# A hybrid encoder step on one core: the first norm moved onto the token-major rows, and the residual turned beside the first gate

## Chip, core and metric

The kernel runs on one NeuronCore of a Trainium2 chip. TensorE (PE) multiplies matrices and transposes, VectorE (DVE), ScalarE (ACT) and GpSimd (POOL) work elementwise, and SyncE (SP) issues nearly all DMAs. The metric is the device time of one execution in microseconds (us). All data are float32; products are made from operands split into a high and a low float32r part.

## What is computed

One step of one layer over 336 tokens (16 meta tokens, 256 of a prompt, 64 of a sample), each a row of 2048 numbers:

```python
u = _rmsnorm(x, norm_mix_w)
z_a, xbc_a, dt_a, qkv_b, z_b, beta_b, a_b, gate_a, gate_b = jnp.split(u @ w_in, SPLIT_IDX, axis=-1)
# ya: SSD mixer with causal conv; ob: gated DeltaNet with causal conv; both chunked scans
mix = (jax.nn.sigmoid(gate_a) * (ya.astype(xd) @ w_out[:SSD_D_INNER])
       + jax.nn.sigmoid(gate_b) * (ob.astype(xd) @ w_out[SSD_D_INNER:]))
h = x + mix
hid = jnp.square(jax.nn.relu(_rmsnorm(h, norm_mlp_w) @ w_up))
h = h + hid @ w_down
```

where `_rmsnorm` divides each token's row by its root mean square and multiplies by a weight per channel. Conv and scan states come out too, and the rows of `h` after a last norm.

## The kernel before

**Layout.** `u` is kept channel-major: 16 tiles `k` of 128 channels (partitions) by 336 tokens, as a high part `uh` and a low part `ul`. The weights stream past it: `w_in`, then `w_out`, `w_up`, `w_down`, in chunks `n` of 512 rows by 256 columns (`raw`, 512 KB each, three buffers). `wload(n)` issues the DMA of a chunk three chunks ahead, `wsplit(n)` makes `hi` on ACT and `lo = raw - hi` on DVE (for chunk 3 on POOL). The buffer of chunk n+3 is free when `lo` of chunk n is done. `block` multiplies two column tiles of 128 by `u`: four chunks, in each 4 `k` by 2 columns by 3 products (hi·uh, lo·uh, hi·ul), into two PSUM tiles `pbig`. So one block over `u` is 96 products of 336 columns.

**Order.** PE runs its instructions in the order in which the code issues them. From `manual` to `manual.close()` all engines do. Elsewhere a scheduler orders the other engines and the DMA queue of SP ahead of time; each engine then runs its fixed list, and SP stands still at a DMA whose condition isn't met, with all later DMAs behind it. The DMAs share eight completion counters in turn, so a DMA also waits until the eighth before it has landed.

**Start.** The token rows come as three tiles `x0` to `x2` of 112 rows by 2048. For each, a sum of squares (`sumsq`) and a root (`root`, its power on POOL) give one factor per token; PE transposes the raw `x` (`flip`, 48 transposes of 112 columns) into `xT`. The factors are spread over all partitions by three small products (`prx`, `rbx`), each `k` is scaled from `xT` into `ut` (`u_scale`, DVE and POOL by turns) and split with the norm weight (`u_split`: `uh` on ACT, `ul` on DVE). The first block runs beside this, two generator steps for each `k`.

**Behind the first block** come, in PE's order, six transposes `pcol` of conv weights and states (`cra`, `crb`, `sra`, `srb`) and 32 products `ptok` with the 64 columns for time step, beta and decay (`wt`, loaded by two DMAs of 128-byte runs, split into `wtr` by ACT and DVE). The loads `cra` to `wt` go into the pool `sp`, which is opened when `xp`, the pool of `x0` to `x2`, is closed, in the same space. So they wait for the last reader of `x`. `dvec` (two DMAs of 4-byte elements, 64 by 16) has its own space. `scratch` writes the channel-major residual from `xT` to DRAM (`xTd`, 16 DMAs of 160 KB) and zeroes four DRAM scratch tensors (`aD`, `uD`, 12 DMAs of 258 KB) that the second mixer's scans use, from about 580 us on.

**First gate.** Beside the first scan of the second mixer (`scan_gdn(0)`), `gate_a` runs 8 blocks. For each of 16 tiles it reads `xTd` back (`xr`), takes the sigmoid on ACT, multiplies by `acc` on DVE, adds `xr` on POOL, and stores to `hAd`, where `gate_b` takes it later.

Of the kernel before, what the change touches and what calls it, by code (L numbers as in the profile page):

```python
# [42 lines left out]
def tile_hybrid_step(ctx: ExitStack, tc: tile.TileContext, i: dict, o: dict):  # L43
    nc = tc.nc
# [9 lines left out]
    def scr(name):  # L54
        return pss.tile([P, 512], F32, tag="sc", name=name)

    def mm(out, lhsT, rhs, start=True, stop=True, **kw):
        nc.tensor.matmul(out, lhsT=lhsT, rhs=rhs, start=start, stop=stop, **kw)  # L58

    def act(out, in_, func=AF.Copy, **kw):  # L60
        nc.scalar.activation(out=out, in_=in_, func=func, **kw)  # L61

    def tt(eng, out, a, b, op):
        eng.tensor_tensor(out=out, in0=a, in1=b, op=op)  # L64

    def stt(out, a, s, b, op0, op1):
        nc.vector.scalar_tensor_tensor(out=out, in0=a, scalar=s, in1=b, op0=op0, op1=op1)  # L67

    V, G = nc.vector, nc.gpsimd
# [15 lines left out]
    def transp(out, in_):  # L85
        n = in_.shape[0]
        nc.tensor.transpose(out, in_, ident[:n, :n])
# [32 lines left out]
    NM, SN, NP_, CB_, GN = 0, 16, 32, 48, 72  # L120

    rowd = dpool.tile([2, 48, NT], F32, name="rowd")
    xTd = dpool.tile([KD, P, NO], F32, name="xTd")
    hAd = dpool.tile([KD, P, NO], F32, name="hAd")

    DG = P * P + P
# [66 lines left out]
    def wload(n):  # L193
        if n >= len(stream) or n in raws:
            return
        raw = wpool.tile([P, 4, 256], F32, tag="raw", name="raw", bufs=3)
        for c0, src in stream[n]:
            nc.sync.dma_start(raw[:, :, c0:c0 + src.shape[1]], src.rearrange("(k p) c -> p k c", p=P))
        raws[n] = raw

    def wsplit(n):
        if n >= len(stream) or n in split:
            return
        wload(n)
        hi = wpool.tile([P, 4, 256], F32R, tag="hi", name="hi", bufs=3)
        act(hi, raws[n])
        lo = wpool.tile([P, 4, 256], F32R, tag="lo", name="lo", bufs=3)
        tt(G if n == 3 else V, lo, raws[n], hi.bitcast(F32), SUB)
        split[n] = hi, lo

    used, hold = [0], [len(stream)]
# [46 lines left out]
    def proj(n0=0, n1=None):  # L258
        return (yield from block(KD, umov, (n0, n0 if n1 is None else n1), NT))
# [25 lines left out]
        G.memset(t, 0.0)  # L285
    xctx = ExitStack()
    xp = xctx.enter_context(tc.tile_pool(name="xp", bufs=1))
    xs = []
    segs = [[(0, "meta", 0, 16), (16, "pr", 0, 96)], [(0, "pr", 96, 112)], [(0, "pr", 208, 48), (48, "sa", 0, 64)]]
    src = {"meta": i["meta_tokens"], "pr": i["x_prompt"][0], "sa": i["x_sample"][0]}  # L290
    def load_x(n):
        for p0, s, r0, nr in segs[n]:
            nc.sync.dma_start(xs[n][p0:p0 + nr, :], src[s][r0:r0 + nr, :])

    for n in range(3):
        xs.append(xp.tile([112, D], F32, name=f"x{n}"))
    load_x(0)
    load_x(1)
    prow = sp0.tile([73, P], F32, name="prow")
    for r0, name, nr in ((NM, "norm_mix_w", 16), (SN, "ssd_norm_w", 16), (NP_, "norm_mlp_w", 16), (CB_, "ssd_conv_b", 24), (GN, "gdn_norm_w", 1)):  # L300
        nc.sync.dma_start(prow[r0:r0 + nr, :], i[name][0].rearrange("(t c) -> t c", c=P))
    load_x(2)
    warm = sp0.tile([P, 1], F32, name="warm")
    act(warm, ones[:, 0:1], AF.Square)

    def load_cols(dst, row, n):
        ps = scr("pcol")
        transp(ps[:, :n], row[:n, :])
        V.tensor_copy(dst, ps[:, :n])


    xT = [cpool.tile([P, 4, NT], F32, tag=t, name="xT", bufs=b) for t, b in (("q", 2), ("k", 2), ("v", 1))]
    xT.append(sp0.tile([P, 4, NT], F32, name="xT3"))
    junk = acc.rearrange("p k n -> p (k n)")[:112, :]
    ssx = sp0.tile([112, 4], F32, name="ssx")
    rsx = sp0.tile([112, 3], F32, name="rsx")
    dgx = sp0.tile([112, 3, 112], F32, name="dgx")
    rbx = sp0.tile([P, NT], F32, name="rbx")
    HD = D // 2

    def sumsq(f, x, d0, n):
        d = junk[:, d0:d0 + x.shape[1]]
        if f is act:
            act(d, x, AF.Square, accum_out=ssx[:, n:n + 1])
        else:
            V.scalar_tensor_tensor(out=d, in0=x, scalar=1.0, in1=x, op0=MUL, op1=MUL, accum_out=ssx[:, n:n + 1])

    def flip(n, k):
        ps = scr("pu").rearrange("p (k t) -> p k t", k=4)[:, :, :112]
        for m in range(4):  # L330
            transp(ps[:, m, :], xs[n][:, (k + m) * P:(k + m + 1) * P])
        return xT[k // 4][:, :, n * 112:(n + 1) * 112], ps

    def root(n):
        r = rsx[:, n:n + 1]
        V.tensor_scalar(out=r, in0=ssx[:, n:n + 1], scalar1=1.0 / D, scalar2=EPS, op0=MUL, op1=ADD)
        tt(G, r, r, nhalf_pow[:112, 0:1], ALU.pow)

    def spread_d(n):
        V.tensor_scalar(out=dgx[:, n, :], in0=ident[:112, :112], scalar1=rsx[:, n:n + 1], scalar2=None, op0=MUL)  # L340

    manual = ExitStack()
    manual.enter_context(tc.manual_schedule())

    pw_ = scr("pwarm")
    for n in range(8):
        mm(pw_[:, :P], ident, ident)
    prx = psb.tile([P, 512], F32, tag="big", name="prx")
    sumsq(act, xs[0], 0, 0)
    for k in range(0, KD, 4):  # L350
        (V.tensor_copy if k < 8 else act)(*flip(0, k))
    root(0)
    sumsq(V, xs[1], D, 1)
    for k in range(0, KD, 4):
        act(*flip(1, k))
    root(1)
    load_cols(par, prow, 73)
    for n in range(3):
        wload(n)
    sumsq(act, xs[2][:, :HD], 0, 2)  # L360
    sumsq(V, xs[2][:, HD:], D, 3)
    tt(V, ssx[:, 2:3], ssx[:, 2:3], ssx[:, 3:4], ADD)
    root(2)
    spread_d(0)
    spread_d(1)
    act(*flip(2, 0))
    late = [flip(2, k) for k in (4, 8, 12)]
    spread_d(2)
    wsplit(0)
    for n in range(3):  # L370
        mm(prx[:, n * 112:(n + 1) * 112], ones[:112, :], dgx[:, n, :])
    act(rbx, prx[:, :NT])
    for a in late:
        act(*a)
    xctx.close()
    sp = start.enter_context(tc.tile_pool(name="sp", bufs=1))

    ut = {}

    def u_scale(k):  # L380
        ut[k] = sp0.tile([P, NT], F32, tag="ut", name="ut", bufs=6)
        tt(G if k % 2 else V, ut[k], xT[k // 4][:, k % 4, :], rbx, MUL)

    def u_split(k):
        t, w = ut.pop(k), par[:, NM + k:NM + k + 1]
        act(uh[:, k, :], t, AF.Copy, scale=w)
        stt(ul[:, k, :], t, w, uh[:, k, :].bitcast(F32), MUL, SUB)

    def ctile(tag, name, bufs):
        return cpool.tile([P, 4, NT], F32, tag=tag, name=name, bufs=bufs)

    def ftile(name):
        return fpool.tile([P, 340], F32, tag="c", name=name, bufs=NC_)[:, :NO]
# [63 lines left out]

    main0 = kept(proj_ssd(0), tiles0)  # L460
    hold[0] = 0
    for k in range(4):
        u_scale(k)
    for k in range(KD):
        u_split(k)
        if k + 4 < KD:
            u_scale(k + 4)
        if k % 4 == 1 and k < KD - 4:
            wsplit(k // 4 + 1)
        for _ in range(2 if k < KD - 1 else 1):  # L470
            next(main0)
    manual.close()
# [522 lines left out]

    def scratch():

        for k in range(KD):
            nc.sync.dma_start(xTd[k], xT[k // 4][:, k % 4, NMETA:])
            yield 1.0  # L1000
        for n in range(2):
            for t in (aD, uD):
                for c in range(3):
                    nc.sync.dma_start(t[n][c].rearrange("h (p r) -> (h p) r", r=4 * DG // P), zero)

    def chain(*gens):
        for g in gens:
# [2 lines left out]
    def gate_a():  # L1010
        done = []

        def store():
            nc.sync.dma_start(hAd[done[0][0]], done.pop(0)[1])

        for b in range(8):
            pt = yield from proj(NMETA)
            for j in range(2):
                k = b * 2 + j
                xr = ftile("xr")  # L1020
                nc.sync.dma_start(xr, xTd[k])
                sgt = ftile("sgt")
                act(sgt, pt[j][:, :NO], AF.Sigmoid)
                tt(V, sgt, sgt, acc[:, k, :], MUL)
                tt(G, sgt, sgt, xr, ADD)
                done.append((k, sgt))
                if len(done) > 1:
                    store()
        store()
# [221 lines left out]
```

## Time and profile before

| | us |
|---|---|
| three runs | 2331.46, 2333.14, 2334.69 |
| median | 2333.14 |
| the profiled execution: its own time | 2331.78 |
| span, from the first to the last instruction | 2330.1 |
| TensorE's mean granted clock | 0.994 of full speed |

The profile is of one execution, and its times count from the start of the span. The page gives busy times and the groups of instructions. The chain that ended last is followed back from the last instruction, and its pieces stand in order of time. The stretches give busy times and the granted clock between two times. The timelines list instructions with their start and length, and "idle before" with what ended it. A matmul's length overlaps with the next one's; what one costs is the distance of two starts. Of TensorE's clock a row shows 1.00 (2.4 GHz) or 0.50 (1.2 GHz).

### The profile page before, as it was taken

The numbers are of one execution on the slowest core, as the hardware profiler recorded it, in microseconds if no ns is written. First come the engines' busy times: TensorE is split into PE (matmuls) and PEld (weight loads), VectorE is DVE, ScalarE is ACT, GpSimd is POOL, SyncE is SP. The second block draws the span as 40 slices with busy tenths as digits, with TensorE's granted clock in tenths as the row PEclk, the third lists the DMA queues.
The fourth block names the chain that finished last, engine by engine and source line by source line (L and its number), as shares of the span: only waits on it lengthen the run. The fifth ranks groups of instructions, "written<-read, shape, count | busy, mean of one in ns | idle before, by whom it ended". The sixth has DMA issues, their size and how long they took to land.

```text
span 2330.1 us, 40632 instructions
## 1 busy us (share of the span) xinstructions
PE 2300.5 (99%) x16393; PEld 2278.1 (98%) x16393; DVE 1360.9 (58%) x2147; ACT 1064.6 (46%) x1830; POOL 333.0 (14%) x488
## 2 busy tenths in 40 slices
PE   7999999999999999999999999999999999999997
PEld 7999999999999999999999999999999999999997
DVE  6674858585865547658668467444444444444444
ACT  5655546455445545554554445433343244324433
POOL 3151505041211102212212110000000000000000
PEclk8999999999999999999999999999999999999999
DMA  7846555545575555555546644544554444445543
GB/s 194 225 121 188 143 159 150 159 135 173 156 200 170 148 164 139 154 150 144 156 148 165 170 142 145 154 149 151 148 154 149 150 148 151 154 146 153 168 141 117
DMA packets 411046, 362.87 MB, mean 156 GB/s; under 512 B 48329, under 2 KB 407834, under 8 KB 410394
## 3 DMA queue, kind: packets, MB, share of 16 engines
q1 hardware_dynamic: 410746, 360.15, 53.1%
q8 instruction: 128, 2.10, 0.4%
q14 instruction: 60, 0.49, 0.1%
q10 hardware_dynamic: 112, 0.13, 0.0%
HBM read 340.57 MB, written 19.66 MB: 155 GB/s over the span
## 4 chain that ended last, share of the span: by engine, by line
PE 91%; DVE 5%; DMA 2%; issue 1%; SPq 1%; ACT 0%; ACTq 0%; POOL 0%; DVEq 0%
PE pbig L58 84%; DVE lo L64 1%; PE po L58 1%; DMA em<-rowd 1%; DVE pr L64 1%; DVE ubt L858 1%; PE pS L58 0%; PE pw L58 0%; PE pyd L58 0%; DVE c L67 0%; PE pkk L58 0%; PE pqk L58 0%; PE ph L58 0%; DMA x<-in_x_sample_dram 0%; PE pyo L58 0%
## 5 line engine op out<-in xcount | busy, mean ns | idle before, releaser
L64 DVE TENSOR_TENSOR lo<-raw,hi 128x1024 fp32r<-128x1024 f32 x591 | 739.1, 1251 | 697.3 <-ACT hi L61 688.0
L61 ACT ACTIVATE hi<-raw 128x1024 fp32r<-128x1024 f32 x592 | 626.3, 1058 | 892.1 <-PE pbig L58 834.6
L58 PE MATMUL pbig<-uh,hi 128*128 128x320 f32 (+2 forms) x2176 | 688.9, 317 | 3.1 <-ACT uh L61 3.1
L58 PE MATMUL pbig<-ul,hi 128*128 128x320 f32 (+2 forms) x2176 | 681.9, 313 | 2.9 <-DVE ul L67 2.7
L58 PE MATMUL pbig<-uh,lo 128*128 128x320 f32 (+2 forms) x2176 | 680.8, 313 | 1.6 <-DVE lo L64 1.6
L58 PEld LDWEIGHTS pbig<-uh,hi 128*128 128x128 f32 x2176 | 410.9, 189 | 9.1 <-ACT uh L61 3.8
L58 PEld LDWEIGHTS pbig<-ul,hi 128*128 128x128 f32 x2176 | 410.8, 189 | 4.7 <-DVE ul L67 4.3
L58 PEld LDWEIGHTS pbig<-uh,lo 128*128 128x128 f32 x2176 | 411.0, 189 | 2.4 <-DVE lo L64 2.4
L58 PE MATMUL pbig<-hh,hi 128*128 128x320 f32 x1024 | 318.0, 311 | 0.0
L58 PE MATMUL pbig<-hnl,hi 128*128 128x320 f32 x1024 | 317.1, 310 | 0.0
L58 PE MATMUL pbig<-hl,hi 128*128 128x320 f32 x1024 | 316.3, 309 | 0.0
L58 PE MATMUL pbig<-hh,lo 128*128 128x320 f32 x1024 | 316.2, 309 | 0.0
L58 PE MATMUL pbig<-hnh,lo 128*128 128x320 f32 x1024 | 315.8, 308 | 0.0
L58 PE MATMUL pbig<-hnh,hi 128*128 128x320 f32 x1024 | 315.1, 308 | 0.0
L58 PEld LDWEIGHTS pbig<-hnh,lo 128*128 128x128 f32 x1024 | 192.9, 188 | 0.0
L58 PEld LDWEIGHTS pbig<-hl,hi 128*128 128x128 f32 x1024 | 192.6, 188 | 0.0
L58 PEld LDWEIGHTS pbig<-hh,hi 128*128 128x128 f32 x1024 | 192.6, 188 | 0.0
L58 PEld LDWEIGHTS pbig<-hnh,hi 128*128 128x128 f32 x1024 | 192.4, 188 | 0.2
L58 PEld LDWEIGHTS pbig<-hh,lo 128*128 128x128 f32 x1024 | 192.5, 188 | 0.0
L58 PEld LDWEIGHTS pbig<-hnl,hi 128*128 128x128 f32 x1024 | 192.2, 188 | 0.0
L58 PE MATMUL pbig<-yh,hi 128*128 128x320 f32 x512 | 161.1, 315 | 0.0
L58 PE MATMUL pbig<-yh,lo 128*128 128x320 f32 x512 | 157.5, 308 | 0.0
(303 smaller groups left out, 2425.8 us busy)
## 6 DMA issues: line engine op xcount, KB each, us to landing
raw<-in_w_in_dram SPq DMA_DIRECT2D x256, 512.0 KB, 3.8
raw<-in_w_up_dram SPq DMA_DIRECT2D x128, 512.0 KB, 3.8
raw<-in_w_down_dram SPq DMA_DIRECT2D x128, 512.0 KB, 3.4
raw<-in_w_out_dram SPq DMA_DIRECT2D x64, 512.0 KB, 3.4
raw<-in_w_in_dram SPq DMA_DIRECT2D x32, 256.0 KB, 3.1
em<-rowd SPq DMA_DIRECT2D x8, 512.0 KB
u<-uD SPq DMA_DIRECT2D x4, 768.0 KB, 7.1
eab<-rowd SPq DMA_DIRECT2D x8, 336.0 KB, 6.9
```

The lines of the kernel that those rows point to most:

```text
L58: nc.tensor.matmul(out, lhsT=lhsT, rhs=rhs, start=start, stop=stop, **kw)
L61: nc.scalar.activation(out=out, in_=in_, func=func, **kw)
L64: eng.tensor_tensor(out=out, in0=a, in1=b, op=op)
L858: V.tensor_reduce(out=ubt[:NE, j0:, s], in_=v, axis=AX.X, op=ADD)
```

## The change

The norm is made in place on the rows of `x`, before the transposes. `scale(n, q)` multiplies a quarter (512 columns) of `x` tile `n` by the factor of each token, `x0` on ACT, `x1` and `x2` on DVE. `u_tile(k)` transposes the three scaled pieces of tile `k` into one PSUM tile and makes `uh` and `ul` from it. Three tiles are made before the first block; the others are made in it, three tiles ahead of the products. `xT`, `ut`, `rbx`, `prx` and `xTd` go. The rows of norm weights (`prow`) are loaded from ACT's queue. Ten products on the identity and four of 512 columns on raw `x` stand ahead on PE (`warmer`). `lo` of chunk 3 moves from POOL to DVE. `xp` is closed, and `sp` opened, after the 31 steps of the first block instead of before them. In `gate_a` each block loads its 256 columns of the raw rows again (three DMAs into `xr`), transposes them on PE (six transposes for each block), and DVE adds them from PSUM in place of POOL.

```diff
-        tt(G if n == 3 else V, lo, raws[n], hi.bitcast(F32), SUB)
+        tt(V, lo, raws[n], hi.bitcast(F32), SUB)
...
+        nc.scalar.dma_start(prow[r0:r0 + nr, :], i[name][0].rearrange("(t c) -> t c", c=P))
+    for n in range(3):
         for p0, s, r0, nr in segs[n]:
             nc.sync.dma_start(xs[n][p0:p0 + nr, :], src[s][r0:r0 + nr, :])
     for n in range(3):
+        wload(n)
...
+    def warmer(n, mov):
+        ps = scr("pwarm")
+        for _ in range(n):
+            mm(ps[:, :mov.shape[1]], ident[:mov.shape[0], :], mov)
...
+    def scale(n, q):
+        x, r = xs[n][:, q * QD:(q + 1) * QD], rsx[:, n:n + 1]
+        if n == 0:
+            act(x, x, AF.Copy, scale=r)
+        else:
+            V.tensor_scalar(out=x, in0=x, scalar1=r, scalar2=None, op0=MUL)
+
+    def u_tile(k):
+        ps = scr("pu")
+        for n in range(3):
+            transp(ps[:, n * XW:(n + 1) * XW], xs[n][:, k * P:(k + 1) * P])
+        w = par[:, NM + k:NM + k + 1]
+        act(uh[:, k, :], ps[:, :NT], AF.Copy, scale=w)
+        stt(ul[:, k, :], ps[:, :NT], w, uh[:, k, :].bitcast(F32), MUL, SUB)
...
-    xctx.close()
-    sp = start.enter_context(tc.tile_pool(name="sp", bufs=1))
...
+    LEAD = 3
+    warmer(10, ident)
+    for n in range(2):
+        warmer(2, xs[n][:, 3 * QD:])
+    sumsq(0)
+    root(0)
+    sumsq(1)
+    scale(0, 0)
+    root(1)
+    sumsq(2)
+    scale(1, 0)
+    root(2)
+    load_cols(par, prow, 73)
+    wsplit(0)
+    scale(2, 0)
+    for k in range(LEAD):
+        u_tile(k)
     for k in range(KD):
-        u_split(k)
-        if k + 4 < KD:
-            u_scale(k + 4)
+        if k % 4 == 0 and k < KD - 4:
+            for n in range(3):
+                scale(n, k // 4 + 1)
+        if k + LEAD < KD:
+            u_tile(k + LEAD)
+        for _ in range(2 if k < KD - 1 else 1):
+            next(main0)
         if k % 4 == 1 and k < KD - 4:
             wsplit(k // 4 + 1)
-        for _ in range(2 if k < KD - 1 else 1):
-            next(main0)
     manual.close()
+    xctx.close()
+    sp = start.enter_context(tc.tile_pool(name="sp", bufs=1))
...
-        for k in range(KD):
-            nc.sync.dma_start(xTd[k], xT[k // 4][:, k % 4, NMETA:])
-            yield 1.0
         for n in range(2):
             for t in (aD, uD):
                 for c in range(3):
                     nc.sync.dma_start(t[n][c].rearrange("h (p r) -> (h p) r", r=4 * DG // P), zero)
+                    yield 1.0
...
+            xr = ctile("qk"[b % 2], "xr", 2).rearrange("p k n -> p (k n)")
+            for m, (src_, r0, n) in enumerate(rows):
+                nc.sync.dma_start(xr[:n, m * 256:(m + 1) * 256], src_[r0:r0 + n, b * 256:(b + 1) * 256])
             pt = yield from proj(NMETA)
             for j in range(2):
                 k = b * 2 + j
-                xr = ftile("xr")
-                nc.sync.dma_start(xr, xTd[k])
+                px = scr("px")
+                for m, (_, _, n) in enumerate(rows):
+                    transp(px[:, m * P:m * P + n], xr[:n, m * 256 + j * P:m * 256 + (j + 1) * P])
                 sgt = ftile("sgt")
                 act(sgt, pt[j][:, :NO], AF.Sigmoid)
                 tt(V, sgt, sgt, acc[:, k, :], MUL)
-                tt(G, sgt, sgt, xr, ADD)
+                tt(V, sgt, sgt, px[:, :NO], ADD)
```

The scheduler also orders SP's list anew. Before, from the second `dvec` on, SP's queue in the first block reads:

```order
L488 DMA dvec<-in_ssd_d_dram 64x16x1
L490 DMA pb<-in_ssd_dt_bias_dram 128x32
L198 DMA raw<-in_w_in_dram 128x4x256
L491 DMA pb<-in_gdn_dt_bias_dram 128x16
L492 DMA pb<-in_ssd_a_log_dram 128x32
L493 DMA pb<-in_gdn_a_log_dram 128x16
L503 DMA wt<-in_w_in_dram 128x16x32
L198 DMA raw<-in_w_in_dram 128x4x256
L504 DMA wt<-in_w_in_dram 128x16x32
L198 DMA raw<-in_w_in_dram 128x4x256
```

The first `dvec`, `cra`, chunk 3 (`raw`), `crb`, `sra` and `srb` stand ahead of these rows, and the 16 `xTd` and 12 zeroing DMAs behind them. In the changed kernel the same queue reads, from behind chunks 0 to 2 on:

```order
L469 DMA dvec<-in_ssd_d_dram 64x16x1 x2
L197 DMA raw<-in_w_in_dram 128x4x256
L982 DMA aD_106<-zero 128x516 x3
L982 DMA uD_108<-zero 128x516 x3
L982 DMA aD_107<-zero 128x516
L197 DMA raw<-in_w_in_dram 128x4x256
L982 DMA aD_107<-zero 128x516 x2
L982 DMA uD_109<-zero 128x516 x2
L197 DMA raw<-in_w_in_dram 128x4x256
L982 DMA uD_109<-zero 128x516
L197 DMA raw<-in_w_in_dram 128x4x256
L457 DMA cra<-in_ssd_conv_w_dram 96x128
```

Both `dvec` now stand ahead of chunk 3 (the first `raw` here), and all 12 zeroing DMAs and chunks 4 to 6 ahead of `cra`; `crb`, `sra`, `srb`, four `pb` and both `wt` follow it, 12 DMAs in all.

On PE, the first products before and what stands ahead of them:

```order
L87 MATMUL pu<-ident,x_147 128x112 x16
L58 MATMUL prx<-dgx,ones 128x112 x3
L58 MATMUL pbig<-uh,hi 128x336
L58 MATMUL pbig<-uh,lo 128x336
L58 MATMUL pbig<-ul,hi 128x336
```

In the changed kernel 12 transposes stand ahead of the first product, and three (of `x0`, `x1`, `x2`) ahead of each later group of six, 12 times:

```order
L58 MATMUL pbig<-uh,hi 128x336
L58 MATMUL pbig<-uh,lo 128x336
L58 MATMUL pbig<-ul,hi 128x336
L87 MATMUL pu<-ident,x_144 128x112
L87 MATMUL pu<-ident,x_145 128x112
L87 MATMUL pu<-ident,x_146 128x112
L58 MATMUL pbig<-uh,hi 128x336
```

The transposes that stood in one piece ahead of the block now stand between its products. `pcol` and `ptok` follow the block in both.

## Rows read from the trace of the kernel before

**Rows 1.** The page, parts 1 and 4: busy time of engines; shares of the chain

```profile
PE 2300.5 (99%) x16393; PEld 2278.1 (98%) x16393; DVE 1360.9 (58%) x2147; ACT 1064.6 (46%) x1830; POOL 333.0 (14%) x488
...
PE 91%; DVE 5%; DMA 2%; issue 1%; SPq 1%; ACT 0%; ACTq 0%; POOL 0%; DVEq 0%
```

**Rows 2.** The chain that ended last, to 54 us: start, length, what

```profile
6.89 8.00 DMA x<-in_x_sample_dram
...
16.59 0.95 ACT hi L61
...
17.57 1.24 DVE lo L64
...
40.03 5.85 DMA wt<-in_w_in_dram
...
46.65 1.29 DVE wtr L64 x2
...
48.59 4.99 PE ptok L58 x32
```

**Rows 3.** Timeline of PE, 15 to 26 us: start, length, instruction, idle before

```profile
15.03 3.22 PE L87 MATMUL pu<-ident,x 112*128 112x112 f32 x16 [2.58 <-DMA x<-in_x_sample_dram]
...
21.84 0.65 PE L58 MATMUL pbig<-uh,hi 128*128 128x336 f32 x1 [2.30 <-ACT uh L61]
...
25.54 0.48 PE L58 MATMUL pbig<-ul,hi 128*128 128x336 f32 x1
25.82 0.48 PE L58 MATMUL pbig<-uh,hi 128*128 128x336 f32 x1
```

**Rows 4.** Stretches of the first block: length, busy us (count), PEclk, DMA, GB/s

```profile
21.84:28.20 6.36, 6.12 (x19) 5.26 (x20) 6.36 (x9) 5.19 (x9) 4.09 (x4) 0.50 0.43 117
28.20:38.50 10.30, 7.62 (x48) 7.06 (x47) 10.30 (x11) 3.04 (x5) 7.40 (x5) 1.00 0.18 43
38.50:45.20 6.70, 5.95 (x22) 5.41 (x21) 2.76 (x7) 2.11 (x5) 0.00 (x0) 0.50 1.11 189
```

**Rows 5.** Operations on DVE in the first block, and a scaling at the kernel's end

```profile
L67 DVE SCALAR_TENSOR_TENSOR ul<-ut,par,uh 128x336 fp32r<-128x336 f32 x16 | 12.3, 798 | 2.6 <-ACT uh L61 2.4
...
L1217 DVE TENSOR_SCALAR yt<-yt,frs x3: 748/752/753, 2319.2 to 2320.7; 128x1024 f32<-128x1024 f32 x2, 64x1024 f32<-64x1024 f32 x1
```

**Rows 6.** Timeline of SP's queue: start, length, DMA

```profile
11.60 0.69 SPq L488 DMA_DIRECT2D dvec<-in_ssd_d_dram  x1
...
26.45 0.61 SPq L488 DMA_DIRECT2D dvec<-in_ssd_d_dram  x1
...
28.28 0.39 SPq L198 DMA_DIRECT2D raw<-in_w_in_dram  x1
```

**Rows 7.** DMA: `dvec` to landing; packets of 28.4:36, 45.5:52 and 56:60

```profile
DMA to landing us min/median/max: 12.0/13.4/14.8
...
DMA packets 809, 0.01 MB, mean 1 GB/s; under 512 B 803, under 2 KB 809, under 8 KB 809
...
DMA packets 2229, 2.48 MB, mean 382 GB/s; under 512 B 210, under 2 KB 2229, under 8 KB 2229
...
DMA packets 1510, 1.02 MB, mean 255 GB/s; under 512 B 42, under 2 KB 1505, under 8 KB 1509
```

**Rows 8.** Timeline of PE at 684 us: four transposes between products

```profile
684.07 0.60 PE L87 MATMUL pv<-ident,v 128*80 128x128 f32 x4
684.42 0.39 PE L58 MATMUL pbig<-uh,hi 128*128 128x320 f32 x1
684.65 0.31 PE L58 MATMUL pbig<-ul,hi 128*128 128x320 f32 x1
684.80 0.31 PE L58 MATMUL pbig<-uh,lo 128*128 128x320 f32 x1
```

**Rows 9.** The first gate: a stretch (columns as in rows 4); a wait of PE

```profile
627.00:660.00 33.00, 33.00 (x228) 33.00 (x227) 30.91 (x46) 15.36 (x20) 6.64 (x5) 1.00 0.65 189
...
PE pbig L58 <- DVE lo L64: 0.2, 1, 0.2
```

More of the change, by code (lines that the diff above doesn't have):

```diff
@@ L122, in tile_hybrid_step @@
     rowd = dpool.tile([2, 48, NT], F32, name="rowd")
-    xTd = dpool.tile([KD, P, NO], F32, name="xTd")
     hAd = dpool.tile([KD, P, NO], F32, name="hAd")
@@ L287, in tile_hybrid_step @@
     xp = xctx.enter_context(tc.tile_pool(name="xp", bufs=1))
-    xs = []
+    XW = NT // 3
     segs = [[(0, "meta", 0, 16), (16, "pr", 0, 96)], [(0, "pr", 96, 112)], [(0, "pr", 208, 48), (48, "sa", 0, 64)]]
     src = {"meta": i["meta_tokens"], "pr": i["x_prompt"][0], "sa": i["x_sample"][0]}
-    def load_x(n):
+    xs = [xp.tile([XW, D], F32, name=f"x{n}") for n in range(3)]
+    HD, QD = D // 2, D // 4
+    manual = ExitStack()
+    manual.enter_context(tc.manual_schedule())
+    warm = sp0.tile([P, 1], F32, name="warm")
+    act(warm, ones[:, 0:1], AF.Square)
+    prow = sp0.tile([73, P], F32, name="prow")
+    for r0, name, nr in ((NM, "norm_mix_w", 16), (SN, "ssd_norm_w", 16), (NP_, "norm_mlp_w", 16), (CB_, "ssd_conv_b", 24), (GN, "gdn_norm_w", 1)):
+        nc.scalar.dma_start(prow[r0:r0 + nr, :], i[name][0].rearrange("(t c) -> t c", c=P))
+    for n in range(3):
         for p0, s, r0, nr in segs[n]:
@@ L295, in tile_hybrid_step @@
     for n in range(3):
[L296 to L304, printed above, removed]
+        wload(n)
     def load_cols(dst, row, n):
@@ L309, in load_cols @@
         V.tensor_copy(dst, ps[:, :n])
[L312 to L332, printed above, removed]
+    def warmer(n, mov):
+        ps = scr("pwarm")
+        for _ in range(n):
+            mm(ps[:, :mov.shape[1]], ident[:mov.shape[0], :], mov)
+    junk = acc.rearrange("p k n -> p (k n)")[:XW, :]
+    ssx = sp0.tile([XW, 6], F32, name="ssx")
@@ L334, in root, with sumsq @@
+    rsx = sp0.tile([XW, 3], F32, name="rsx")
+    def sumsq(n):
+        for m in range(2):
+            x, d, t = xs[n][:, m * HD:(m + 1) * HD], junk[:, m * HD:(m + 1) * HD], ssx[:, 2 * n + m:2 * n + m + 1]
+            if m == 0:
+                act(d, x, AF.Square, accum_out=t)
+            else:
+                V.scalar_tensor_tensor(out=d, in0=x, scalar=1.0, in1=x, op0=MUL, op1=MUL, accum_out=t)
     def root(n):
         r = rsx[:, n:n + 1]
-        V.tensor_scalar(out=r, in0=ssx[:, n:n + 1], scalar1=1.0 / D, scalar2=EPS, op0=MUL, op1=ADD)
@@ L337, in root @@
[L337 to L371, printed above, removed]
@@ L372, in tile_hybrid_step @@
-    act(rbx, prx[:, :NT])
-    for a in late:
-        act(*a)
-    xctx.close()
-    sp = start.enter_context(tc.tile_pool(name="sp", bufs=1))
[L378 to L387, printed above, removed]
+        tt(V, r, ssx[:, 2 * n:2 * n + 1], ssx[:, 2 * n + 1:2 * n + 2], ADD)
@@ new lines, in root @@
+        V.tensor_scalar(out=r, in0=r, scalar1=1.0 / D, scalar2=EPS, op0=MUL, op1=ADD)
+        tt(G, r, r, nhalf_pow[:XW, 0:1], ALU.pow)
+    def scale(n, q):
+        x, r = xs[n][:, q * QD:(q + 1) * QD], rsx[:, n:n + 1]
+        if n == 0:
+            act(x, x, AF.Copy, scale=r)
+        else:
+            V.tensor_scalar(out=x, in0=x, scalar1=r, scalar2=None, op0=MUL)
[6 more added lines that the diff above has]
+        stt(ul[:, k, :], ps[:, :NT], w, uh[:, k, :].bitcast(F32), MUL, SUB)
@@ L461, in tile_hybrid_step @@
     hold[0] = 0
-    for k in range(4):
-        u_scale(k)
-    for k in range(KD):
-        u_split(k)
-        if k + 4 < KD:
-            u_scale(k + 4)
+    LEAD = 3
[15 more added lines that the diff above has]
+        u_tile(k)
+    for k in range(KD):
+        if k % 4 == 0 and k < KD - 4:
[5 more added lines that the diff above has]
+            next(main0)
         if k % 4 == 1 and k < KD - 4:
             wsplit(k // 4 + 1)
-        for _ in range(2 if k < KD - 1 else 1):
-            next(main0)
     manual.close()
+    xctx.close()
+    sp = start.enter_context(tc.tile_pool(name="sp", bufs=1))
     hold[0] = len(stream)
@@ L1014, in store @@
             nc.sync.dma_start(hAd[done[0][0]], done.pop(0)[1])
+        rows = [(i["x_prompt"][0], 0, P), (i["x_prompt"][0], P, P), (i["x_sample"][0], 0, NSA)]
         for b in range(8):
+            xr = ctile("qk"[b % 2], "xr", 2).rearrange("p k n -> p (k n)")
+            for m, (src_, r0, n) in enumerate(rows):
+                nc.sync.dma_start(xr[:n, m * 256:(m + 1) * 256], src_[r0:r0 + n, b * 256:(b + 1) * 256])
             pt = yield from proj(NMETA)
```

## The prediction

> **What bounds the kernel now.** I read the page first. PE is busy 99% of the span and makes up 91% of the chain that ended last [rows 1], so nearly every microsecond outside PE is free, and two kinds of places count: those where PE waits, and those where PE itself gets more or less to do. The chain in order of time then shows that waits stand only at the start. Up to 14.89 us it is the loading of `x` (6.89 + 8.00), and at the end of the first block it is `wt`: issued at 40.03, landed at 45.88 (40.03 + 5.85), split by 47.94 (46.65 + 1.29); then, behind the last `pcol`, `ptok` starts at 48.59 and takes 4.99 [rows 2]. From there on the chain is PE's own work. So the first thing to ask of a change at the start is not when the first block ends but when `ptok` starts.
>
> The timeline and the stretches show the block in between. Its first product starts at 21.84, 6.95 us after `x` has landed [rows 2, 3]. The clock is at 0.50 for 6.36 us, at 1.00 for 10.30, and at 0.50 again for 6.70 [rows 4]. A product of 336 columns costs 0.28 us at half clock (25.54 to 25.82) [rows 3] and 0.156 at full clock (4.99 / 32) [rows 2].
>
> **The change, part by part.**
>
> *Until the first product.* The bytes of `x` are the same, and the last DMA of `x` had been issued 3 us before the second tile landed, so I leave its landing at 14.9. Behind it come, as before, half sums of squares, a root, and `hi` and `lo` of chunk 0, which before were done at 18.81 (17.57 + 1.24) [rows 2]; I leave that at 18.4, as DVE's sum is no longer. Behind `lo` on DVE stands the scaling of `x2`'s quarter: half of the 0.75 of 1024 columns, 0.4 [rows 5]. That is 18.8. Then the last transpose of tile 0 and nine more ahead of the first product, at 3.22 / 16 = 0.2 us each: 20.8 [rows 3]. Gain: 1 us, between 0 and 3.
>
> *The first block.* Each `k` costs six products and, for 12 of them, three transposes: 6 x 0.28 + 3 x 0.2 = 2.3 us at half clock. At full clock a transpose costs 0.11: four of them delay the second product behind them from 684.07 + 0.15 to 684.65, by 0.43 [rows 8]. So 6 x 0.156 + 3 x 0.11 = 1.27. DVE needs less for a `k`: one `ul` (0.8 beside a busy POOL, which now has nothing there), a quarter of a `lo` (0.3) and half a scaling (0.2), at most 1.3 [rows 2, 5]. So PE is dense and I take the first stretch of rows 4 for the clock: 6.4 us at half, then full. That is 2.8 `k` by 27.2, the 12th by 38.9, the last by 42.6. Before, PE was at half clock in this block until 45.20 [rows 4], so the block itself could end some 4 us earlier.
>
> *What it waits for then.* The order of SP decides, and it is worse. Chunk 3, needed at `k` = 12, stands behind both `dvec`. What those cost is in the trace: the first, issued at 11.60, landed 14.8 us later, at 26.4, and the second, issued at 26.45, needed 12.0 [rows 6, 7]. Between 28.4 and 36.0 the DMA engines moved 809 packets, 803 of them under 512 bytes, and 0.01 MB in all, although a weight chunk had been issued at 28.28 [rows 6, 7]. That is 106 small packets for each us, so a `dvec` of 64 x 16 = 1024 elements takes 9.6 us, and what is queued behind it doesn't move. Two in a row from 17 us, when chunks 0 to 2 are nearly in, end at 36. Chunk 3 lands at 37, its `hi` and `lo` (0.95 + 1.24) [rows 2] are done at 39.3, and the block ends at 43.
>
> Behind chunk 3 there are 12 zeroing DMAs (258 KB each, 3.2 MB) and chunks 4 to 6 (1.6 MB) ahead of `cra`: 4.8 MB. At 382 GB/s [rows 7] that is 12.5 us, so `cra` lands at about 49.5. At 255 GB/s, another stretch of the same rows, it is 19 us. Eleven more DMAs follow, the two `wt` last. They are issued by about 51.2: each issue takes some half a microsecond [rows 6], and the eighth before it must have landed. With 5.85 us from issue to landing, and 1.3 for the split of the first half (0.65 on DVE, as much on ACT), `ptok` starts at 58.4 instead of 48.6 [rows 2]. **Loss: 9.8 us.** Bounds: if nothing were in the way of SP's list, `cra` would still wait for the last transposes of `x` and for chunk 6, whose buffer comes free with `lo` of chunk 3, so 38.5 at the best. Then 12 issues, 5.2 us, and 5.85 and 1.3 give 50.8, a loss of 2.2. With 255 GB/s the loss is 16.
>
> [...]
>
> *The clock behind it.* PE has almost nothing from 43 to 58. Before, PE waited 2.3 us in front of the first product and began at half clock, and stayed there for 6.36 us [rows 3, 4]. So `ptok` begins at half clock: in 6.4 us it makes 23 products, which took 3.6 before. **Loss: 2.8 us**; none if the wait is short, 3.3 at most from the 6.70 of the other stretch.
>
> *The first gate.* PE gets 48 transposes, 32 of 128 columns and 16 of 64, in a part where it has no gap: 33.00 of 33.00 us busy, one wait of 0.2 us for `lo` [rows 9]. 48 x 0.11 = 5.2; the short ones may cost half, 4.3. I take **4.8 us**. At the half clock's 0.2 it would be 9.6, but the clock is at 1.00 there. DVE gets 16 adds of 320 columns, at the price of a `ul` without POOL beside it, about 0.5 us each, over eight blocks; in its densest part (30.91 of 33.00 us) [rows 9] some five of them, 2.4 us, against 2.1 free and the POOL adds that go. I count nothing, as `lo` is made up to two chunks ahead; where that cover is gone, PE waits what DVE is late. What POOL no longer does (16 adds, `lo` of chunk 3) and what DMA no longer moves (`xTd`, both ways) was beside PE, and gives nothing.
>
> For the price of a transpose the page TensorE: Matmul & The Clock Gate of the Trainium skill (section Back-to-back issue gap) gives columns / 2.4 GHz + 2.5 ns: 56 ns for 128 columns. By that estimate the gate would cost 2.3 us instead of 4.8; the 0.11 of the row, measured between products of this kernel, decides.
>
> *Sum.* 9.8 + 2.8 + 4.8 = 17.4 us. The gain of the earlier block is in the first term and is used up in the wait. The profiled execution took 2331.78 us, so 2349.2 is the same execution after the change. The median of the runs is 1.36 above it: **2350**.
>
> **Rivals.**
>
> *The queue clears early.* The small loads don't hold the others up when two stand together, or engines that are done early pass the zeroing on. Then the loss is the 2.2 us that SP's list costs anyhow, plus the clock, plus the gate: 2.2 + 2.8 + 4.8 = 9.8, or 2343. For it: the first `dvec` shared the queue with loads ahead of it and behind it, and no row shows how long it stood alone. Against it: the empty stretch from 28.4 to 36.
>
> *Not slower: the dense start keeps the clock.* If the ten plus four products on PE before the block bring it to 1.00 from the first product on, 16 `k` cost 12 x 1.27 + 4 x 0.94 = 19 us, and the block ends at 39.8. If `wt` too is there by then, `ptok` starts at about 40.5, 8 us earlier than before, and with the gate's 4.8 the sum is -3.3: 2330. It decides at `wt`: landed before 40 or not. For it: the block before lost some 6 us to half clock [rows 4]. Against it: PE has nothing to do from its products on `x1` to the landing of `x2`, and `cra` can't be issued before the last transposes.
>
> *The gate stalls.* The `xr` rows come on SP's list, behind stores that wait for DVE, and a weight chunk behind them is late; each of 8 blocks waits a microsecond or two. That adds about 10: 2360. Against it: before, the same list held the same stores, and PE waited 0.2 us.
>
> **How the numbers follow.** Forecast 0.60, early queue 0.17, stalls in the gate 0.05, the dense start 0.18. A measurement of this kernel can tell about 0.2%, 4.7 us, from no change. The dense start comes out within that (2330) in 0.10 and beyond it, with a cheaper gate, in 0.08. So slower 0.82, same 0.10, faster 0.08. The forecast's own bounds: 2.2 + 0 + 4.3 above 2333 is 2340, 16 + 3.3 + 5.2 is 2358. The range runs from 2336 to 2359; it takes in the early queue and leaves out the dense start.
>
> **What would show it.** In the profile after: the first product at about 21, the block's last at 43, hardly any bytes on the DMA engines from 19 to 35 us, a wait of `pcol` for `cra` until about 50, `ptok` at about 58 with 0.28 us from product to product, and 48 `px` transposes that add 5 us between 625 and 760 with no new wait. I am wrong if `wt` lands before 45, or if the stretch of 4-byte packets is not there.

## The result, and the profile after

The changed kernel takes 2356.11 us (median of four runs, 2355.13 to 2357.35) against 2333.39 of the kernel before: 1.0102 times as long, with an interval of 1.0089 to 1.0114, or 22.7 us more. The forecast was 16.6 more, with 2359 as its upper end. The profiled execution took 2355.54 us, its span 2353.4; before, the span was 2330.1 [rows 1]. So 23.3 us of span are to be found.

The waits of PE over the whole span (what waited, for what, us in total, times, longest) show where PE stands that didn't before:

```profile
PE pcol L87 <- DMA cra<-in_ssd_conv_w_dram: 7.6, 1, 7.6
PE ptok L58 <- DVE wtr L64: 7.3, 1, 7.3
...
PE pbig L58 <- ACT hi L61: 2.1, 1, 2.1
...
PE pbig L58 <- DVE lo L64: 1.6, 2, 0.8
...
PE pcum L58 <- DVE la L64: 1.0, 1, 1.0
```

The first four are in the first block and behind it. (PE also waits 6.3 us for the scaling of `x`, but ahead of the first product, which comes at 21.06 and not at 21.84 [rows 3], so nothing is lost there.) Two times 7 us are waits for loads that SP issues, one behind the other, from its list: `cra`, then `wt`. The stretches (length, busy us and counts by engine, granted clock, DMA share, GB/s) and SP's own timeline (start, us, what it issues) show why these come late:

```profile
19.00:25.00 6.00, 5.74 (x29) 5.68 (x29) 3.73 (x8) 3.98 (x7) 0.00 (x0) 0.56 0.05 0
25.00:31.00 6.00, 6.00 (x47) 5.93 (x45) 4.66 (x8) 4.34 (x8) 0.00 (x0) 1.00 0.05 0
...
36.00:42.00 6.00, 3.06 (x18) 2.60 (x17) 2.44 (x4) 2.35 (x4) 0.00 (x0) 0.94 0.98 332
42.00:48.00 6.00, 3.73 (x16) 3.45 (x15) 0.22 (x1) 0.51 (x2) 0.32 (x2) 0.77 1.00 307
48.00:54.00 6.00, 0.66 (x4) 0.57 (x4) 0.23 (x2) 0.00 (x0) 0.00 (x0) 0.51 0.69 210
```

```profile
18.83 0.40 SPq L197 DMA_DIRECT2D raw<-in_w_in_dram  x1
19.33 15.44 SPq L982 DMA_DIRECT2D aD<-zero  x3
...
46.26 0.33 SPq L457 DMA_DIRECT2D cra<-in_ssd_conv_w_dram  x1
...
54.40 0.43 SPq L484 DMA_DIRECT2D wt<-in_w_in_dram  x1
54.88 1.88 SPq L485 DMA_DIRECT2D wt<-in_w_in_dram  x1
```

The DMA queues from 19 to 31 us (packets, MB):

```profile
DMA packets 1284, 0.01 MB, mean 0 GB/s; under 512 B 1284, under 2 KB 1284, under 8 KB 1284
```

For 12 us, while PE is busy with the block, 0 GB/s arrive; 1,284 packets, all under 512 bytes, are all that moves then. SP stands for 15.44 us at three zeroing loads. Then the bytes that were kept back come at 307 to 332 GB/s, with chunk 3 first among them, and `cra` and `wt` behind. The chain of waits (start, us, what) goes through the same places up to `ptok`:

```profile
19.33 9.41 SPq L982
...
45.21 7.84 DMA raw<-in_w_in_dram
...
54.88 5.51 DMA wt<-in_w_in_dram
...
61.88 6.69 PE ptok L58 x32
```

`ptok` starts at 61.88 and ends at 68.57; before, 48.59 and 53.58 [rows 2]. That is 15.0 of the 23.3: 13.3 of start, and 1.7 because `ptok` begins at half clock (0.50 from 61.88 to 64 us). The wait of `pcum` adds 1.0: the first `sgt` of the gate is at 648.76 instead of 632.72, 16.04 later. From there to the last `sgt` these are the stretches of the kernel before and of the changed one:

```profile
632.72:754.08 121.36, 120.47 (x962) 118.01 (x961) 75.70 (x117) 56.97 (x99) 24.83 (x27) 1.00 0.65 184
```

```profile
648.76:776.89 128.13, 128.12 (x1003) 122.50 (x1001) 76.83 (x132) 57.33 (x99) 5.57 (x12) 1.00 0.61 172
```

They differ by 6.8, and the eighth pair of tiles has its transposes behind the last `sgt`. 15.0 + 1.0 + 6.8 is 22.8; from the last `sgt` to the end it is 0.5 more, the eighth pair among them.

In the timeline of PE at the second pair of the gate the price can be read:

```profile
664.11 0.31 PE L58 MATMUL pbig<-uh,lo 128*128 128x320 f32 x1
664.25 1.15 PE L87 MATMUL px<-ident,xr 128*128 128x128 f32 x6
665.34 0.42 PE L58 MATMUL pbig<-uh,hi 128*128 128x320 f32 x1
665.60 0.31 PE L58 MATMUL pbig<-ul,hi 128*128 128x320 f32 x1
```

From 664.11 to 665.60 is 1.49 us; two products at their pace of 0.147 (one start to the next) are 0.29. Six transposes cost 1.20, not the 0.66 of the forecast. The weight loads in between have a gap in front of the first short one and of the last:

```profile
664.56 0.40 PEld L87 LDWEIGHTS px<-ident,xr 64*128 64x128 f32 x3 [0.17 <-issue]
665.13 0.14 PEld L87 LDWEIGHTS px<-ident,xr 64*128 64x128 f32 x1 [0.17 <-issue]
```

### The profile page after: what moved, and what is told of

It is laid out like the page before. It is cut to its first block, busy times and chain, and to the rows that moved or that the text cites. A ratio compares the mean times of both kernels' runs of the same rounds, so it can differ in the third digit from the quotient of the medians.

```text
span 2353.4 us, 40726 instructions
## 1 busy us (share of the span) xinstructions
PE 2310.6 (98%) x16447; PEld 2283.0 (97%) x16447; DVE 1356.0 (58%) x2163; ACT 1064.2 (45%) x1825; POOL 301.5 (13%) x463
## 4 chain that ended last, share of the span: by engine, by line
PE 93%; DVE 3%; DMA 2%; SPq 1%; ACT 0%; issue 0%; POOL 0%; ACTq 0%; DVEq 0%; POOLq 0%
PE pbig L58 86%; PE po L58 1%; SPq L982 1%; DMA raw<-in_w_in_dram 1%; DVE lo L64 1%; DVE c L67 1%; PE pS L58 0%; DMA em<-rowd 0%; PE pw L58 0%; PE pyd L58 0%; PE ph L58 0%; PE pkk L58 0%; PE pqk L58 0%; PE px L87 0%; PE pyo L58 0%; DMA uD<-zero 0%
```

## The experiments

Two questions: what keeps `wt` back (the small packets of `dvec`, the bytes of the zeroing, or the place on SP's list), and what the gate costs. Ratios are to the kernel before, which took 2332.89 us beside the first four runs, 2332.45 beside the next four and 2333.31 beside the last two.

**`dvec` in one load** (e1).

```diff
-    for h in range(2):
-        nc.sync.dma_start(dvec[h * 64:(h + 1) * 64, :], i["ssd_d"][0].rearrange("(t h) -> h t", h=2)[h].partition_broadcast(64))
+    dv = sp0.tile([P, 32], F32, name="dv")
+    nc.sync.dma_start(dv, i["ssd_d"][0].partition_broadcast(P))
+    for h in range(2):
+        G.tensor_copy(dvec[h * 64:(h + 1) * 64, :], dv[h * 64:(h + 1) * 64, :].rearrange("p (t h) -> p t h", h=2)[:, :, h])
```

> The changed kernel, but the two loads of `dvec` (64 x 16 elements of 4 bytes each) are one load of 128 rows of 32 elements and two small POOL copies. Theory (the two `dvec` hold SP's queue; in the changed kernel the bytes stop from 19 to 31 us and SP stands 15.44 us at the first zeroing load): chunk 3 lands by 25 instead of 38.4, PE no longer waits 2.10 and 0.84 us for its `hi` and `lo`, the first block ends at about 42.5 instead of 45.4, `wt` is issued at about 45 instead of 54.88, and `ptok` starts at 51 to 53 instead of 61.88. Time 2346 (2344 to 2349) against 2356.1. Rival (the queue is held by the 3.2 MB of zeroing and by the weight chunks, `dvec` only shares it): only the 2.9 us of waits inside the block go, `ptok` starts at 59 or later, and the time is 2353 or more.

Measured: 2344.83 us (2343.36 to 2346.61), ratio 1.0055 (1.0038 to 1.0072); 11.3 less than the changed kernel. PE's waits of 2.10 and 0.84 us for `hi` and `lo` of chunk 3 are gone, and the block's last product starts at 40.15 instead of 45.41. SP's list and the stretch from 19 to 25 us now read:

```profile
18.91 0.38 SPq L197 DMA_DIRECT2D raw<-in_w_in_dram  x1
19.35 0.97 SPq L984 DMA_DIRECT2D aD<-zero  x2
```

```profile
19.00:25.00 6.00, 5.66 (x30) 5.59 (x31) 3.81 (x8) 3.96 (x7) 0.38 (x2) 0.63 0.86 279
```

The two zeroing loads are issued in 0.97 us where three took 15.44, and 279 GB/s arrive where there were none. So the small packets of `dvec`, 8 KB in all, cost the changed kernel 11.3 us. `ptok` starts at 49.29, earlier than expected, but it takes 7.40 us: it begins at half clock and stays there longer than in the changed kernel, where it took 6.69, although PE stood still for less long ahead of it (7.0 us, there 7.6 and 7.3). Why, no run shows. The chain:

```profile
36.33 4.26 DMA raw<-in_w_in_dram
...
42.42 5.38 DMA wt<-in_w_in_dram
...
49.29 7.40 PE ptok L58 x32
```

What is left is the place: `cra` is issued at 37.24, when the last transposes of `x` have been made, and the others to `wt` behind it (e5 and e6 test this).

**The zeroing behind `ptok`** (e2).

```diff
-    zero = sp0.tile([P, 4 * DG // P], F32, name="zero")
...
-    for t in (tok, zero, acs):
+    for t in (tok, acs):
         G.memset(t, 0.0)
...
+    zero = sp.tile([P, 4 * DG // P], F32, name="zero")
+    tt(G, zero, tokT[:, 0:1].to_broadcast([P, 4 * DG // P]), tokT[:, 0:1].to_broadcast([P, 4 * DG // P]), SUB)
```

> The changed kernel, but the tile of zeros is made from `tokT`, so that the 12 zeroing loads (3.2 MB) can't be issued before `ptok`; `dvec` is as in the changed kernel. Theory (`dvec` holds the queue until about 35 us, the zeroing costs SP's list the rest): the bytes still stop from 19 to 31 us and PE still waits 2 to 3 us for chunk 3, but `cra` is issued at about 41.5 instead of 46.26, the last `wt` at 47 instead of 54.88, and `ptok` starts at about 53.7 instead of 61.88. Time 2348 (2346 to 2352). Rival one (only `dvec` counts): `cra` stays where it is, gain under 3 us, 2353 or more. Rival two (the 3.2 MB are only put off, and then keep weight chunks behind `ptok` waiting): new waits for `raw` between 60 and 90 us, and 2354 or more.

Measured: 2349.22 us (2347.88 to 2352.19), ratio 1.0073 (1.0058 to 1.0088). `cra` is issued at 42.43, the last `wt` at 47.86, and `ptok` starts at 55.08 (expected 41.5, 47 and 53.7). The bytes still stop from 19 to 31 us. Thus the zeroing is a cause beside `dvec`, worth 7 us in the changed kernel; of the second rival's waits behind `ptok` there are none. The gains of e1 and e2, 11.3 and 6.9, are together more than the 16.0 that the start and `pcum` lost: both shorten the same wait, and they can't be added.

**Five transposes for a pair** (e3).

```diff
-            for m, (src_, r0, n) in enumerate(rows):
+            for m, (src_, r0, n) in enumerate(rows[:2]):
                 nc.sync.dma_start(xr[:n, m * 256:(m + 1) * 256], src_[r0:r0 + n, b * 256:(b + 1) * 256])
+            for j in range(2):
+                nc.sync.dma_start(xr[j * 64:(j + 1) * 64, 512:640], rows[2][0][:, b * 256 + j * P:b * 256 + (j + 1) * P])
...
+                if j == 0:
+                    transp(px[:, 256:384], xr[:, 512:640])
...
```

DVE adds the stacked columns by themselves for every second tile.

> The changed kernel, but the 64 sample rows of a block's two column halves are loaded one above the other, so that a block turns them with one transpose of 128 rows instead of two of 64 rows: five per block instead of six, none of them short; DVE gets one more add of 64 columns per block. In the changed kernel six transposes delay the product behind them by 1.20 us (664.11 to 665.60, less two products of 0.147), where four long ones of the kernel before cost 0.43. Theory A (the step between 128 and 64 rows stops PE: the weight loads stand 0.17 us at 664.56 and at 665.13): five cost 0.55, gain 8 x 0.65 = 5.2, time 2351 (2350 to 2352). Theory B (each transpose costs 0.2 here, whatever its rows): gain 8 x 0.2 = 1.6, time 2354.5.

Measured: 2351.37 us (2351.08 to 2353.17), ratio 1.0082 (1.0067 to 1.0097); 4.7 less than the changed kernel. The timeline of PE at the same place:

```profile
663.79 0.31 PE L58 MATMUL pbig<-uh,lo 128*128 128x320 f32 x1
663.94 0.71 PE L87 MATMUL px<-ident,xr 128*128 128x128 f32 x5
664.40 0.39 PE L58 MATMUL pbig<-uh,hi 128*128 128x320 f32 x1
664.63 0.31 PE L58 MATMUL pbig<-ul,hi 128*128 128x320 f32 x1
```

664.63 - 663.79 - 0.29 = 0.55 for five, 0.11 each, as theory A had it. Two short ones cost 1.20 - 4 x 0.11 = 0.76 in the changed kernel, 0.38 each, with the steps from 128 rows to 64 and back: a transpose of 64 rows between others of 128 costs more than three long ones. The page TensorEngine Tiling (Array Packing) of the Trainium skill, section Key Properties, says that a change of the tiling mode, not of the tile alone, drains the engine. The 0.17 us in which the weight loads stand there would fit with it, but no run here tells the drain from another cost of that step. Not every change in the number of rows costs this: ahead of `ptok` in the kernel before, transposes of 96 and 72 rows stand by turns behind products of 128, and their starts are 0.08 apart:

```profile
46.63 0.25 PE L87 MATMUL pcol<-ident,cra 96*128 96x96 f32 x1
46.71 0.23 PE L87 MATMUL pcol<-ident,sra 72*128 72x72 f32 x1
46.78 0.25 PE L87 MATMUL pcol<-ident,crb 96*128 96x96 f32 x1
```

The saving is a bit under 5.2: DVE's added adds bring a new wait, `pks` for `sgt`, of 1.0 us.

**The gate without transposes** (e4).

```diff
+            G.memset(xr[64:, 512:], 0.0)
...
-                px = scr("px")
-                for m, (_, _, n) in enumerate(rows):
-                    transp(px[:, m * P:m * P + n], xr[:n, m * 256 + j * P:m * 256 + (j + 1) * P])
...
-                tt(V, sgt, sgt, px[:, :NO], ADD)
+                tt(V, sgt, sgt, xr[:, :NO], ADD)
```

> The changed kernel without the 48 transposes of the residual in the first gate: the rows of `x` are loaded as before, and 320 columns of them are added as they lie, so the residual that is added is another one. The difference to the changed kernel is the price of the transposes. From the two traces: the last `sgt` of the gate starts 22.8 us later than before, the first one 16.0, and one more pair of transposes lies behind it, so 7 to 8 us and a time of 2348.5. By the prediction (0.11 each, 4.8 in all): 2351.3. By 1.20 for each of eight pairs of tiles, 9.6 in all: 2346.5.

Measured: 2345.74 us (2344.23 to 2347.34), ratio 1.0057 (1.0042 to 1.0072). The 48 transposes cost 10.4, nearest to the 9.6 of eight times 1.20, and more than twice the forecast's 4.8. The stretch between the first and the last `sgt`, which holds seven of the eight pairs:

```profile
647.90:767.50 119.60, 119.60 (x962) 117.82 (x962) 76.57 (x132) 54.52 (x99) 10.29 (x18) 1.00 0.65 184
```

128.13 - 119.60 = 8.5, or 1.22 a pair. It also shows why the two traces differ by less: the gate of the kernel before took 121.36, 1.8 more than this one, of which 0.9 are waits of PE that the new gate doesn't have; where the other 0.9 go stays open.

**The small loads in places of their own** (e5), in the same way for `crb`, `sra`, `srb` and `pb`.

```diff
-    cra = sp.tile([96, P], F32, name="cra")
+    cra = sp0.tile([96, P], F32, name="cra")
...
-    wt = sp.tile([P, KD, 64], F32, name="wt")
+    wt = sp0.tile([P, KD, 64], F32, name="wt")
```

> The changed kernel, but `cra`, `crb`, `sra`, `srb`, `pb` and `wt` have places of their own, so their loads don't wait for the last transposes of `x`: on SP's list chunk 3 then stands ahead of `dvec` and the zeroing behind `wt`; `dvec` is still in small packets. Theory (`dvec` holds what is behind it on the queue for some 19 us, but not what is ahead): chunk 3 lands by 25, PE doesn't wait for it, the block ends at 42.5, `dvec` is through at 41 to 43, `wt` lands at 45 to 46 and `ptok` starts at about 47.5 instead of 61.88. Time 2341.5 (2339 to 2345). Rival (the place of `wt` on the list doesn't matter, what matters are the bytes): `ptok` later than 55, 2349 or more.

Measured: 2344.81 us (2344.77 to 2345.49), ratio 1.0052 (1.0037 to 1.0068). The time is within the bounds, but the way there was not the expected one: `ptok` starts at 54.4, not at 47.5. The chain:

```profile
37.11 12.32 DMA wt<-in_w_in_dram
...
49.53 0.07 ACT wtr L61
...
50.07 0.53 ACT uh L61
...
50.65 2.93 PE pbig L58 x9
```

`wt` is issued at 37.11, behind `dvec`, and lands 12.32 us later. On ACT the split of `wt` stands ahead of the block's last two `uh`, so now PE waits 11.0 us for the first of them inside the block. An earlier place on the list helps by 11.3, but with `dvec` ahead it turns the wait into one inside the block.

**Both** (e6): the edits of e5 and e1.

> As the kernel before it in this list, and `dvec` as one load of 32 contiguous elements per row: nothing is left on the queue that holds it. Theory: `wt` lands before the block's end at 42.5, `ptok` starts at 43.5 and takes 5.0 to 5.3 at full clock, so it ends 20 us earlier than in the changed kernel (68.57): 2336 (2334 to 2339). What is then left of the change's loss is the gate, and the start is some 5 us better than before. Rival (the dense start itself is slower, or the clock falls in the block): the block ends at 45 or later, 2339 or more.

Measured: 2332.43 us (2331.23 to 2333.3), ratio 0.9999 (0.999 to 1.0008); better than expected, and the same as before. The start is what the change could be without the held queue:

```profile
21.00:24.00 3.00, 3.00 (x16) 2.94 (x15) 2.38 (x5) 1.88 (x4) 0.00 (x0) 0.60 0.71 209
24.00:40.20 16.20, 16.20 (x118) 16.05 (x117) 12.55 (x22) 11.08 (x20) 0.39 (x2) 1.00 0.81 196
```

```profile
41.27 4.99 PE ptok L58 x32
```

PE is busy without a gap, the clock is at 1.00 from 24 us on, and `ptok` starts 7.3 us earlier than in the kernel before. The gate takes all of that: from its first `sgt` to its last it needs 128.2 us, as in the changed kernel, and 121.4 in the kernel before.

**All mends** (e7): e1, e2, e3 and e5 together.

> All mends at once: small loads and `wt` in their own places, `dvec` in one load, the zeroing behind `ptok`, and five long transposes for each block of the gate instead of six. Theory: as the kernel without the gate's mend (2336), less the 4.7 that the five transposes gave: 2331.3 (2329 to 2334), so about 2 us below the kernel before. Rival (zeroing behind `ptok` keeps weight chunks waiting): new waits for `raw` from 45 to 80 us, 2334 or more.

Measured: 2328.71 us (2327.21 to 2330.89), ratio 0.9983 (0.9975 to 0.9992), 3.7 us below the kernel before and a little below the expected bounds. `ptok` starts at 41.74; there are no new waits for `raw`; the one of 1.0 us that e3 brought to the gate is there.

**The kernel before, with `dvec` in one load** (e8): the edit of e1 alone.

> The kernel before, with `dvec` as one load of 32 contiguous elements per row and two POOL copies; nothing else. Theory: there the first block ends at 46.47 by its own waits for DVE and ACT, and `ptok` stands at 48.59 for `wt`, so at most 2.1 us go: 2331 (2330.5 to 2333). Rival (the small packets cost the kernel before as much as the changed one): 2325 or less.

Measured: 2327.8 us (2326.1 to 2328.66), ratio 0.9977 (0.9967 to 0.9986): 4.65 less, twice what was expected, and the lowest median of all, though e7 can't be told from it by these runs. The chain:

```profile
42.64 0.42 PE pcol L87 x2
43.06 4.99 PE ptok L58 x32
```

What failed in the theory is that the block of the kernel before ended at 46.47 by its own waits. Its waits of ACT from 30 to 47 us have this row:

```profile
ACT nega L61 <- DMA pb<-in_gdn_a_log_dram: 7.4, 1, 7.4
```

`pb` is behind the second `dvec`, `nega` waits for it and stands on ACT ahead of a `uh`, and PE waits 0.8 for that, up to 41.59. PE is at half clock there from 38.5 to 45.2 [rows 4], so from before that wait on. With one load the wait is gone, and a stretch of the block's end reads:

```profile
36.00:43.00 7.00, 6.86 (x44) 6.42 (x45) 5.89 (x15) 2.64 (x6) 1.46 (x4) 1.00 0.91 294
```

`ptok` starts 5.5 earlier. By the two traces some 2.5 of that is the clock, 0.8 the wait for the `uh`, about 1 a wait of `pcol` for DVE's `cwa` behind the split of `wt`, and 1.2 stands ahead of the first product. Why the clock fell at 38.5 in the one and not in the other no run shows: in both PE has just waited 2.1 us for a `ul`. So the small packets had cost the kernel before, too, in part by a way that stays open; the change put them and the zeroing ahead of more.

**`dvec` on ACT's queue** (e9).

```diff
     for h in range(2):
-        nc.sync.dma_start(dvec[h * 64:(h + 1) * 64, :], i["ssd_d"][0].rearrange("(t h) -> h t", h=2)[h].partition_broadcast(64))
+        nc.scalar.dma_start(dvec[h * 64:(h + 1) * 64, :], i["ssd_d"][0].rearrange("(t h) -> h t", h=2)[h].partition_broadcast(64))
```

> The changed kernel, but the two loads of `dvec`, still 64 x 16 elements of 4 bytes each, are issued by ACT instead of SP; the first stands at the head of ACT's list, the second behind the five `prow`. It tells whether the small packets hold up their own queue or the DMA engines. Theory (the queue alone: in the changed kernel the DMA engines are busy for 0.05 of the time from 19 to 31 us): SP's loads flow, chunk 3 lands by 25, `ptok` starts at 50 as with one load (49.3), 2345 (2343 to 2348). Rival (the small packets take turns on the engines with every other transfer): the landing of `x` or of chunk 3 is late as well, `ptok` starts at 57 or later, 2352 or more.

Measured: 2359.8 us (2358.35 to 2362.02), ratio 1.0115 (1.01 to 1.013). The theory of the own queue falls. SP's timeline, and the DMA queues from 21 to 27 us (packets, MB, share; q10 has the loads of ACT's list):

```profile
1.26 15.27 SPq L302 DMA_DIRECT2D x<-in_x_prompt_dram  x3
...
17.26 9.78 SPq L197 DMA_DIRECT2D raw<-in_w_in_dram  x3
```

```profile
DMA packets 566, 0.00 MB, mean 0 GB/s; under 512 B 566, under 2 KB 566, under 8 KB 566
...
q10 hardware_dynamic: 566, 0.00, 4.2%
```

The small packets are in ACT's queue, and SP's loads, issued since 17.26, don't move: the first of them lands at 33.30. Even the issue of `x` at the start stands for 15 us. The page DMA: Bandwidth & Descriptors of the Trainium skill, section Issuing engines are not separate DMA queues, says that the loads of all engines run on the same 16 DMA engines and interleave. That SP's loads stand while ACT's queue works fits with the first half; of interleaving there is none in these 6 us. What exactly is held (the making of packets, or the engines' own order) no run here shows: the engines are busy for 4.2% of that time.

**The kernel before with the new gate alone** (e10): `gate_a` of the changed kernel, no `xTd`.

> The kernel before with the new first gate alone: `xTd` is neither written nor read, the rows of `x` are loaded again and turned by 48 transposes; the start stays. Theory (six transposes of a pair cost 1.20 us, 9.6 in all, and about 1.8 of that comes back, since the gate of the kernel before has 0.9 us of waits and 0.9 of other losses that the gate without transposes doesn't show: 121.36 us against 119.60): 2332.5 + 8 = 2340.5 (2339.5 to 2342). By the prediction (4.8): 2337.3. If the change's two parts add up, this and the start's 15.0 give the 23 that were measured.

Measured: 2340.3 us (2339.91 to 2341.57), ratio 1.0032 (1.002 to 1.0043): 7.0 more than before, where 8 were expected (the time itself is 0.2 off, since the kernel before took 2333.31 beside it and not 2332.5), and not the 4.8 of the prediction. From the first `sgt` to the last it is 128.1 us, as in the changed kernel. With the 15.0 of the start and the 1.0 of `pcum`, both from the trace, that is 23.0, for the 22.7 that were measured.

## Why the forecast was right, and where it was off

*The direction and the place* were right: the loss stands where the prediction looked for it, at the start of `ptok`, and not in the block. The first product came at 21.06 (20.8 forecast).

*The block.* Forecast to end at 43, it had its last product at 45.4. Its stretches:

```profile
21.00:24.00 3.00, 3.00 (x14) 2.94 (x13) 2.27 (x5) 1.76 (x4) 0.00 (x0) 0.50 0.05 0
24.00:41.00 17.00, 14.06 (x100) 13.47 (x100) 10.12 (x17) 9.92 (x17) 0.00 (x0) 0.99 0.39 126
41.00:45.40 4.40, 4.40 (x19) 4.40 (x20) 1.22 (x3) 0.00 (x0) 0.00 (x0) 0.61 1.04 351
```

The clock rose after 3 us instead of 6.4, which helped; what hurt was that PE waited 2.9 us for chunk 3, in the second of these rows, and then had the lower clock for most of the third, which the forecast didn't have. Without the held queue (e6) the block ended at 40.4, close to the 39.8 of the rival of the dense start, though its clock wasn't 1.00 from the first product on, as that rival had it (0.60 from 21 to 24). It was the queue that decided against this rival, and where it had said: at `wt`.

*The small packets.* The forecast took 106 packets for each us; 1,284 packets in the 12 us from 19 to 31 are 107. From 11.8 to 35 us some 2,040 packets under 512 bytes passed, about as many as the two `dvec` have elements (2 x 1024). Chunk 3 landed at 38.4 (37 forecast). e1 shows the cause. The rival that the queue clears early didn't hold.

*`wt`.* The term of 9.8 was mis-sized: it measured 13.3. Of the 3.5 that were missing, 1.4 are chunk 3. The list behind it was right, its pace wasn't: the bytes came at 332 and 307 GB/s, not at 382, so from chunk 3 to `cra` it took 14.9 us and not 12.5. Chunk 6 was issued at 45.21 and landed at 53.05, `cra` at 53.3, and SP waited for chunk 6 in front of its second `pb`. e2 shows the share of the zeroing.

*The clock behind it.* 1.7 against 2.8, within its bounds; e6, where PE doesn't wait, has 4.99 at full clock.

*The gate.* This term failed: it lies outside its own bounds. 48 x 0.11 took the price of four long transposes and let the short ones "cost half"; the long ones do cost 0.11 (e3), the short ones 0.38. That is 9.6 to 10.4 instead of 4.8 in all. Against the kernel before some 2 come back, so 7 to 8 (e10: 7.0), still outside the bounds of 4.3 to 5.2. That DVE's adds would cost nothing was right: no wait of PE in the gate of the changed kernel.

*Not in the sum*: the 1.0 us in which `pcum` waits for `la`. In e6, where `ptok` comes 20 us earlier, that wait is gone.

Together, in the traces: 13.3 + 1.7 + 1.0 at the start and 6.8 + 0.5 in the gate and behind it, 23.3, where the forecast had 9.8 + 2.8 + 4.8. The forecast of 2350 was 6.1 too low. The time lay in the range because its upper end had been set by the slow bound of the first term, which also covered the gate's miss; that part was luck.

## What to carry to other kernels

Look first at the smallest packets on a list, not at the largest transfers: here two loads of 4 KB, one packet for each element, cost more than 3.2 MB of zeros, and one contiguous load with two small copies on POOL gave 4.65 us to the kernel before and 11.3 to the changed one. When buffers share space with an earlier stage, the loads into them wait for its last reader; give those that the next stage needs their own space, but see what then stands ahead of them on the list (e5 against e6). And price a transpose between products by a row of the same shape, not by its size: here one of 64 rows among long ones was dearer than three long ones, and two of them stacked into one long one were cheap.

## What was not expected of the hardware

- Packets of 4 bytes hold up the loads of another engine's list as well: 566 of them in 6 us on ACT's queue, and 0 bytes of SP's (e9).
- A transpose of 64 rows among transposes and products of 128 costs 0.38 us, a long one 0.11 (e3 against the changed kernel), while steps between 96 and 72 rows cost nothing of the kind (0.08 from start to start).
- In the dense block the clock rose to 1.00 at about 24 us, after ten transposes and 3 us of products without a gap (in e6 a little earlier: 0.60 from 21 to 24). In the kernel before it rose 6.36 us after the first product, with short waits in between [rows 4].
